# Block sums of the Winograd weights: summed on GpSimd, or added up by transfers out of HBM

## The chip, the cores and the metric

The kernel runs on one core of one Trainium2 chip. The metric is device microseconds of that core, from one launch. Three runs of the kernel before took 2677.23, 2677.38 and 2682.13 us; the median is 2677.38 us. Engines are named as in the profile: PE (TensorE), DVE (VectorE), ACT (ScalarE), POOL (GpSimd) and SP (SyncE, which here does nothing but issue transfers).

## The reference, cut to what matters

The model is one step of a two-layer trunk with 128 context and 512 latent tokens (640 columns), width 1024. Each layer is a half-step SwiGLU FFN, a token mixer, and another half-step FFN, so the FFN runs four times. Only the FFN's first two products are touched by the change:

```
def _ffn_half(x, mod, slot, w1, w3, w2, g, b):
    h = _modulate(x, mod[:, 3 * slot], mod[:, 3 * slot + 1])
    f = (jax.nn.silu(h @ w1) * (h @ w3)) @ w2
    return _residual_post_norm(x, f, mod[:, 3 * slot + 2], FFN_RES, g, b)
```

`w1` and `w3` are 1024 x 2816 in fp32, `w2` is 2816 x 1024.

## The kernel before, in words

**Precision.** Every fp32 product is made of three fp32r products: high half of the weight by high half of the activation, high by low, low by high. So each weight block first becomes two tiles: `wh` is the cast on ACT (line 299), `wl` the difference of the fp32 block and `wh` (line 306, called "low" below). Lines 299 and 306 run for each block of 128 x 512 elements, and there are six places (SLOTS) for such pairs of tiles, which go round: a block is cast when the product five places ahead of it is about to be issued, and its place is free once the product before that one has ended.

**The FFN's order.** The 22 column blocks of `w1` and `w3` are taken in chunks of 4, 3, 3, 4, 4 and 4. After each chunk comes a stage with `w2`: eight output blocks, each from as many k-blocks as the chunk has columns. The first three column blocks of an FFN are computed plainly; the other 19 as a *pair* (w1's and w3's block together) in the Strassen-Winograd form. Per FFN that is one pair in the first chunk, three in each of the next two and four in each of the last three, 76 pairs in the whole kernel.

**A pair.** The two weight blocks, each 1024 x 128, are cut into a11, a12 (w1) and a21, a22 (w3), each 512 x 128, or 128 partitions x 512 elements. The activations are cut in the same way and their sums t1 to t4 stand ready for the whole FFN. Seven products take the place of eight: p1 = a11 b11, p2 = a12 b21, p4 = a22 t4, p6 = s2 t2, p7 = s3 t3, p5 = s1 t1, p3 = s4 b22, with the block sums s1 = a21 + a22, s2 = s1 - a11, s3 = a11 - a21, s4 = a12 - s2. Each product is 12 matmuls of 128 x 320. They are issued in the order of the tuple `BLOCKS`: a11, a12, a22, s2, s3, s1, s4.

**Who makes the sums.** `Stream.load` lets SP fetch a pair as two transfers of 512 KB into two raw buffers. `Stream.combine` has POOL make the four sums out of them (line 259) just as the first of them is to be cast; they lie in four buffers `ws` (pool `pt`). The lows of s2 and s4 are made by POOL (`ON_POOL`), all others by DVE.

**What becomes of the products.** `Pair.run` issues the products, and each `prod` ends in `slot()`, which puts on the engines' queues what the products before have left to do. The order on DVE is thus written by hand: m = p1 (a copy on ACT, line 895), the upper left output is m + p2 (line 862, in `c11`), then m + p6, + p7, - p4, + p5 make the lower outputs ("the quarters", line 858 in the trace for all of them), `c12` adds p3, and then come silu, the gate products, and the cast and low of the result (lines 886 and 891), which the `w2` stage reads. Matmul results lie in four single banks of PSUM which go round (p1, p2, p6, p7, p3, and others) and two double ones (p4 with p5).

Every engine works through its queue in order. What waits at the head of a queue holds up all that stands behind it.

## Time and profile before

| | us |
|---|---|
| median of three runs | 2677.38 |
| the profiled execution | 2677.22 |
| its span, first to last instruction | 2675.0 |
| PE busy in it | 2537.6 (95%) |
| DVE busy | 2068.8 (77%) |
| POOL busy | 1243.9 (46%) |
| ACT busy | 1176.7 (44%) |

The clock that was granted to TensorE is 0.983 of full speed as a mean over the span. The profiled execution lasted 2.2 us longer than its span. An engine's idle time costs something only where PE waits for it; the waits of PE are listed by line and by what ended them.

### The profile page before, as it was taken

To read this page: it belongs to the slowest core of one execution; us is meant where nothing else is said; L and a number is where in the kernel's file an instruction comes from. 1 tells how busy PE (TensorE), PEld (TensorE's weight loads), DVE (VectorE), ACT (ScalarE), POOL (GpSimd) and SP (SyncE) were. 2 spreads that over 40 slices of the span, in tenths; PEclk is the share of its full clock that TensorE was granted. 3 is DMA by queue.
4 is the path that set the end of the run, shared out by engine and by line. 5 is a ranking of instruction groups with operands and counts; after the bars stand their busy time and mean duration, and the time that the engine had idled before them with its cause. 6 is when DMAs were issued, how large, how long until landed. Compare 5 with 4: busy or idle time off the path is not lost. (4 is left out here: it accounts for less than half of the span.)

```text
span 2675.0 us, 49819 instructions
## 1 busy us (share of the span) xinstructions
PE 2537.6 (95%) x18662; PEld 2437.0 (91%) x18662; DVE 2068.8 (77%) x3759; ACT 1176.7 (44%) x2596; POOL 1243.9 (46%) x973
## 2 busy tenths in 40 slices
PE   7999999899999999999989999998998999999997
PEld 6999999889778999999989999998996798999997
DVE  6589899856764879988987998898586558777776
ACT  5233333555574533333453333334555735334333
POOL 1345445522444555544565454454234456435554
PEclk9999999999999999999999999998999999999998
DMA  7333332355344233333223333323452331222222
GB/s 266 120 94 107 100 103 91 106 165 148 96 125 156 72 99 99 102 109 104 71 82 99 100 103 109 105 87 125 141 159 80 104 123 44 78 85 84 83 79 72
DMA packets 130544, 285.88 MB, mean 107 GB/s; under 512 B 16832, under 2 KB 34560, under 8 KB 129664
## 3 DMA queue, kind: packets, MB, share of 16 engines
q1 hardware_dynamic: 110720, 247.04, 29.3%
q10 hardware_dynamic: 19584, 35.66, 4.2%
q8 instruction: 148, 2.42, 0.4%
q14 instruction: 92, 0.75, 0.1%
HBM read 254.95 MB, written 8.81 MB: 99 GB/s over the span
## 5 line engine op out<-in xcount | busy, mean ns | idle before, releaser
L306 DVE TENSOR_TENSOR wl<-wr,wh 128x512 fp32r<-128x512 f32 (+1 forms) x524 | 510.0, 987 | 74.2 <-ACT wh L299 73.1
L299 ACT CAST wh<-wr 128x512 fp32r<-128x512 f32 (+1 forms) x570 | 332.7, 607 | 484.5 <-DMA wr<-in_w 309.2
L485 PE MATMUL o<-gh,wh 128*128 128x256 f32 (+1 forms) x1408 | 439.7, 312 | 19.7 <-ACT gh L886 12.1
L485 PE MATMUL o<-gl,wh 128*128 128x256 f32 (+1 forms) x1408 | 438.6, 312 | 1.8
L485 PE MATMUL o<-gh,wl 128*128 128x256 f32 (+1 forms) x1408 | 436.4, 310 | 0.0
L847 PE MATMUL p<-hh,wh 128*128 128x320 f32 x1216 | 377.1, 310 | 10.9 <-DVE pm L858 10.8
L847 PE MATMUL p<-hl,wh 128*128 128x320 f32 x1216 | 377.2, 310 | 6.6 <-DVE hl L1010 6.6
L847 PE MATMUL p<-hh,wl 128*128 128x320 f32 x1216 | 377.4, 310 | 0.7 <-DVE wl L306 0.7
L259 POOL TENSOR_TENSOR ws<-wr 128x512 f32<-128x512 f32 x76 | 110.4, 1453 | 544.8 <-DMA wr<-in_w 508.5
L299 ACT CAST wh<-ws 128x512 fp32r<-128x512 f32 x304 | 185.7, 621 | 355.1 <-PE p L847 128.4
L306 POOL TENSOR_TENSOR wl<-ws,wh 128x512 fp32r<-128x512 f32 x152 | 239.9, 1582 | 189.2 <-ACT wh L299 188.6
L610 DVE SCALAR_TENSOR_TENSOR x<-o,gat,x 128x128 f32<-128x128 f32 (+2 forms) x404 | 193.0, 525 | 137.1 <-PE o L485 135.5
L485 PEld LDWEIGHTS o<-gh,wh 128*128 128x128 f32 x1408 | 267.7, 190 | 23.4 <-ACT gh L886 15.0
L485 PEld LDWEIGHTS o<-gl,wh 128*128 128x128 f32 x1408 | 267.9, 190 | 6.8 <-DVE gl L891 4.8
L485 PEld LDWEIGHTS o<-gh,wl 128*128 128x128 f32 x1408 | 267.5, 190 | 0.0
L847 PEld LDWEIGHTS p<-hh,wh 128*128 128x128 f32 x1216 | 228.9, 188 | 13.2 <-issue 12.2
L847 PEld LDWEIGHTS p<-hl,wh 128*128 128x128 f32 x1216 | 229.1, 188 | 7.7 <-DVE hl L1010 7.7
L847 PEld LDWEIGHTS p<-hh,wl 128*128 128x128 f32 x1216 | 229.2, 189 | 1.8 <-DVE wl L306 1.5
L460 DVE SCALAR_TENSOR_TENSOR scr<-wv,cb 128x512 f32<-128x512 f32 x192 | 174.8, 910 | 0.0
L259 POOL TENSOR_TENSOR ws<-wr,wr 128x512 f32<-128x512 f32 x76 | 130.4, 1715 | 0.6 <-DVE wl L306 0.6
L259 POOL TENSOR_TENSOR ws<-wr,ws 128x512 f32<-128x512 f32 x76 | 130.4, 1716 | 0.0
L306 DVE TENSOR_TENSOR wl<-ws,wh 128x512 fp32r<-128x512 f32 x152 | 129.2, 863 | 0.0
(434 smaller groups left out, 6604.3 us busy)
## 6 DMA issues: line engine op xcount, KB each, us to landing
wr<-in_w SPq DMA_DIRECT2D x176, 512.0 KB, 4.2
wm<-in_wmod ACTq DMA_DIRECT2D x136, 256.0 KB, 3.1
wr<-in_w SPq DMA_DIRECT2D x128, 256.0 KB, 2.7
wv<-in_wmt SPq DMA_DIRECT2D x96, 256.0 KB, 4.1
wm<-in_wmod SPq DMA_DIRECT2D x56, 256.0 KB, 5.3
wr<-in_w SPq DMA_DIRECT2D x64, 192.0 KB, 2.4
wr<-in_wint SPq DMA_DIRECT2D x24, 512.0 KB, 4.3
wr<-in_wo SPq DMA_DIRECT2D x16, 512.0 KB, 3.8
```

The costliest lines, as they stand in the source:

```text
L259: G.tensor_tensor(out=o, in0=x0, in1=x1, op=op)
L299: S.copy(hl[0], src[:, c0:c1])
L306: eng.tensor_tensor(out=t2, in0=src, in1=t.bitcast(F32), op=ALU.subtract)
L460: V.scalar_tensor_tensor(out=scr, in0=w[2 * i + hf], scalar=1.0, in1=cb[:, 2 * st + hf, :], op0=ALU.mult, op1=ALU.mult, accum_out=a[:, 2 * ...
L485: PE.matmul(out[:, :cn], whl[a][:, k, :], b[:, c0:c0 + cn], start=k == 0 and i == 0, stop=k == n - 1 and i == 2)
L610: V.scalar_tensor_tensor(out=c, in0=src, scalar=gat[:, d, s:s + 1], in1=c, op0=ALU.mult, op1=ALU.add)
L847: PE.matmul(out[:, :HN], w[a][:, k, :], b[k][c], start=k == 0 and i == 0, stop=k == 3 and i == 2)
```

## The change

The four block sums are no longer computed by POOL. For each sum, SP copies one 256 KB quarter of the weights out of HBM straight into the sum's buffer, and then POOL issues transfers which add to that buffer: another quarter out of HBM, or the finished s1 out of its buffer. s3 takes a copy and one adding transfer, s1 a copy and one, s2 a copy and one (it adds s1), s4 a copy and two (one out of HBM, then s1). Since the transfers only add, the signs change: s2 = a11 + s1, s3 = a11 + a21, s4 = a12 + a11 + s1; `c12` and the quarters subtract m where they added it. The raw buffers hold only a11 with a12 (512 KB) and a22 (256 KB).

A sum is begun (`begin`) when the same sum of the pair before has been cast and its low made. The first pair of an FFN begins all four when its a11 is cast. All lows are made by DVE. The products follow in the order a11, a12, a22, s3, s1, s2, s4, so p7 and p5 come before p6, and the five quarter operations stand together behind p6. `run_first`, which nothing calls, is dropped.

```diff
-BLOCKS = ("a11", "a12", "a22", "s2", "s3", "s1", "s4")
+BLOCKS = ("a11", "a12", "a22", "s3", "s1", "s2", "s4")
...
             def pair(self, a, b):
                 r = len(self.src)
-                self.src += [(a, (KD, P)), (b, (KD, P))]
+                self.src += [(a, (KD, P)), (b[:, 4:8, :], (4, P))]
+                self.parts[r] = a[:, 0:4, :], a[:, 4:8, :], b[:, 0:4, :], b[:, 4:8, :]
                 return r
...
-            def combine(self, r):
-
-                self.lows()
-                self.load(r + 1)
-                a11, a12 = self.raw[r][:, :512], self.raw[r][:, 512:]
-                a21, a22 = self.raw[r + 1][:, :512], self.raw[r + 1][:, 512:]
-                s1, s2, s3, s4 = (ppt.tile([P, 512], F32, tag="pt", name=f"ws{uid()}") for _ in range(4))
-                for o, x0, x1, op in ((s1, a21, a22, ALU.add), (s2, s1, a11, ALU.subtract), (s3, a11, a21, ALU.subtract),
-                                      (s4, a12, s2, ALU.subtract)):
-                    G.tensor_tensor(out=o, in0=x0, in1=x1, op=op)
-                self.blocks = dict(s1=s1, s2=s2, s3=s3, s4=s4, pair=r)
+            def begin(self, nm, r):
+
+
+                d11, d12, d21, d22 = self.parts[r]
+                o = ppt.tile([P, 512], F32, tag="pt", name=f"ws{uid()}")
+                first = dict(s3=d21, s1=d21, s2=d11, s4=d12)[nm]
+                nc.sync.dma_start(out=o.rearrange("p (a b) -> p a b", b=P), in_=first)
+                for y in dict(s3=(d11,), s1=(d22,), s2=("s1",), s4=(d11, "s1"))[nm]:
+                    if isinstance(y, str):
+                        G.dma_start(out=o, in_=self.sums[r, y], accum_op=ALU.add)
+                    else:
+                        G.dma_start(out=o.rearrange("p (a b) -> p a b", b=P), in_=y, accum_op=ALU.add)
+                self.sums[r, nm] = o
...
-                            if r != self.blocks["pair"]:
-                                self.combine(r)
-                            src = self.blocks[shape]
+                            src = self.sums[r, shape]
+                            if r in self.after:
+                                self.done.append((shape, self.after[r], len(self.w)))
...
+                while self.done and self.done[0][2] < len(self.w):
+                    self.begin(*self.done.pop(0)[:2])
...
-        ON_POOL = ("s2", "s4")
+        ON_POOL = ()
...
+                p7 = bank("p7")
+                self.prod(p7, self.t3)
+                mods(1)
+                self.prod(p5, self.t1)
                 p6 = bank("p6")
...
+                def quarters():
+                    V.tensor_tensor(out=m[:, LO], in0=p6[:, :HN], in1=m[:, LO], op=ALU.subtract)
+                    op(m[:, HI], m[:, LO], p7, ALU.subtract)
                     self.g = u(pe_, f"gf{uid()}")
                     op(self.g[:, LO], m[:, HI], p4, ALU.subtract)
...
                     op(self.g[:, HI], m[:, HI], p5, ALU.add)
                     op(m[:, LO], m[:, LO], p5, ALU.add)
+                    return self.gate1
+                self.prod(p6, self.t2, quarters)
```

POOL, before, over one pair in the middle of the last FFN's last chunk: the sums s1, s2, s3, s4 in that order, then the lows of s2 and s4.

```order
L259 TENSOR_TENSOR ws5770_30189<-wr5744_30032 128x512 [waits DMAHW7_49,Pool_49]
L259 TENSOR_TENSOR ws5771_30190<-ws5770_30189,wr5743_30030 128x512 [waits DMAHW6_49,DVE_49,Pool_49]
L259 TENSOR_TENSOR ws5772_30191<-wr5743_30030,wr5744_30032 128x512 [waits DVE_49]
L259 TENSOR_TENSOR ws5773_30192<-wr5743_30030,ws5771_30190 128x512 [waits Pool_49]
L306 TENSOR_TENSOR wl5777_30202<-ws5771_30190,wh5776_30201 128x512 [waits PE_49,Activation_49]
L306 TENSOR_TENSOR wl5790_30263<-ws5773_30192,wh5789_30262 128x512 [waits PE_49,Activation_49]
```

POOL, now, over one pair there: the adding transfers of s3, s1, s2 and (two) of s4; DMAHW are the counters of SP's transfers, DMASW those of POOL's.

```order
L262 DMA ws5779_30587<-in_w13 128x512 [waits DMAHW2_49,DMASW5_49,DVE_49]
L262 DMA ws5788_30617<-in_w13 128x512 [waits DMASW7_49,DMAHW3_49,DMASW1_49,DVE_49]
L260 DMA ws5791_30638<-ws5788_30617 128x512 [waits DMAHW4_49,DMASW3_49,DVE_49]
L262 DMA ws5795_30660<-in_w13 128x512 [waits DMAHW5_49,DVE_49]
L260 DMA ws5795_30660<-ws5788_30617 128x512 [waits DMASW5_49]
```

Six computing instructions of a pair are gone from POOL and five transfers stand there, each behind a wait for a transfer before it.

SP, now, over two pairs of that chunk: for each pair the copies for s3, s1, s2, s4 of the next one (L257), then the raw blocks (L244). Numbers count up with the allocation, so ws_30469 and ws_30617 are s1 of two pairs that follow each other.

```order
L257 DMA ws_30430<-in_w 128x512 [waits DMASW0_49,DVE_49]
L257 DMA ws_30469<-in_w 128x512 [waits DMASW2_49,DMASW4_49,DMASW1_49,DVE_49]
L257 DMA ws_30488<-in_w 128x512 [waits DVE_49]
L257 DMA ws_30509<-in_w 128x512 [waits DMASW3_49,DVE_49]
L244 DMA wr_30566<-in_w 128x1024 [waits DMAHW2_49,DVE_49]
L244 DMA wr_30568<-in_w 128x512 [waits DMAHW3_49,DVE_49]
L257 DMA ws_30587<-in_w 128x512 [waits DMASW5_49,DVE_49]
L257 DMA ws_30617<-in_w 128x512 [waits DMASW6_49,DMASW7_49,DMASW1_49,DVE_49]
L257 DMA ws_30638<-in_w 128x512 [waits DMAHW6_49,DMAHW4_49,DVE_49]
L257 DMA ws_30660<-in_w 128x512 [waits DMAHW5_49,DMASW0_49,DVE_49]
```

The copy for an s1 waits for three adding transfers of the pair before: the one into its own buffer and the two that read it, of which the last is the second one into s4. SP had only raw blocks to fetch here.

DVE, now, over the end of one pair: the low of the next pair's s3, the five quarters, the low of s1, gate, `c12` (L881), the lows of s2 and s4, the second gate (L889), and `c11` of the next pair.

```order
L312 TENSOR_TENSOR wl5777_30571<-ws5748_30430,wh5776_30570 128x512 [waits DVE_49,DMASW5_49,PE_49,Activation_49]
L921 TENSOR_TENSOR pm5752_30463<-p65773_30564,pm5752_30463 128x320 [waits DVE_49,PE_49]
L866 TENSOR_TENSOR pm5752_30463<-pm5752_30463,p75768_30530 128x320 [waits DVE_49]
L866 TENSOR_TENSOR gf5782_30607<-pm5752_30463,p45763_30507 128x320 [waits DVE_49]
L866 TENSOR_TENSOR gf5782_30607<-pm5752_30463,p45763_30507 128x320
L866 TENSOR_TENSOR pm5752_30463<-pm5752_30463,p45763_30507 128x320
L312 TENSOR_TENSOR wl5781_30591<-ws5757_30469,wh5780_30590 128x512 [waits DMASW6_49,Activation_49]
L866 TENSOR_TENSOR gf5782_30607<-gf5782_30607,sl5767_30528 128x320 [waits DVE_49]
L881 TENSOR_TENSOR sl5767_30528<-p35778_30585,pm5752_30463 128x320 [waits DVE_49,PE_49]
L312 TENSOR_TENSOR wl5790_30621<-ws5760_30488,wh5789_30620 128x512 [waits DMAHW6_49,DMASW7_49,Activation_49]
L312 TENSOR_TENSOR wl5793_30642<-ws5764_30509,wh5792_30641 128x512 [waits DMASW0_49,DMASW1_49,PE_49,Activation_49]
```

Before, the quarters were spread over three products with lows between them, and two of these lows were not on this queue.

## Rows read from the trace of the kernel before

**Rows 1.** The page: busy us (share) and instructions of each engine.

```profile
PE 2537.6 (95%) x18662; PEld 2437.0 (91%) x18662; DVE 2068.8 (77%) x3759; ACT 1176.7 (44%) x2596; POOL 1243.9 (46%) x973
```

**Rows 2.** Whom PE waited for: us in total, times, longest.

```profile
PE o L485 <- ACT gh L886: 12.1, 14, 1.1
...
PE p L847 <- DVE pm L858: 10.8, 6, 1.9
...
PE p L847 <- DVE sl L858: 2.3, 4, 0.8
```

**Rows 3.** The chain that ended last: start us, us, what.

```profile
2544.83 28.11 PE o L485 x192
2572.93 49.27 PE p L847 x336
```

**Rows 4.** Windows (w2 stage, pairs): length; PE, PEld, DVE, ACT, POOL busy; PEclk; DMA share, GB/s.

```profile
2545.00:2573.00 28.00, 28.00 (x193) 28.00 (x192) 14.39 (x28) 6.53 (x13) 6.91 (x5) 1.00 0.32 104
2573.00:2622.00 49.00, 49.00 (x336) 49.00 (x335) 41.73 (x59) 22.36 (x42) 29.64 (x19) 1.00 0.23 70
```

**Rows 5.** Groups by line: POOL's sums and lows; busy, mean ns.

```profile
L306 POOL TENSOR_TENSOR wl<-ws,wh 128x512 fp32r<-128x512 f32 x152 | 239.9, 1582 | 189.2 <-ACT wh L299 188.6
...
L259 POOL TENSOR_TENSOR ws<-wr,ws 128x512 f32<-128x512 f32 x76 | 130.4, 1716 | 0.0
L259 POOL TENSOR_TENSOR ws<-wr,wr 128x512 f32<-128x512 f32 x76 | 130.4, 1715 | 0.6 <-DVE wl L306 0.6
...
L259 POOL TENSOR_TENSOR ws<-ws,wr 128x512 f32<-128x512 f32 x76 | 119.4, 1572 | 6.6 <-POOL ws L259 0.7
...
L259 POOL TENSOR_TENSOR ws<-wr 128x512 f32<-128x512 f32 x76 | 110.4, 1453 | 544.8 <-DMA wr<-in_w 508.5 <-DVE x L610 25.8 <-DVE scr L460 3.4
```

**Rows 6.** DVE's timeline: lows beside POOL's sums and without them.

```profile
2376.82 3.25 DVE L306 TENSOR_TENSOR wl<-wr,wh 128x512 fp32r<-128x512 f32 x2
2379.99 1.91 DVE L891 TENSOR_TENSOR gl<-gf,gh 128x640 fp32r<-128x640 f32 x1
...
2386.84 0.68 DVE L306 TENSOR_TENSOR wl<-ws,wh 128x512 fp32r<-128x512 f32 x1
```

**Rows 7.** POOL's timeline beside those lows.

```profile
2377.89 1.63 POOL L259 TENSOR_TENSOR ws<-ws,wr 128x512 f32<-128x512 f32 x1
```

**Rows 8.** DMA issues: queue, count, KB each, median us from issue to landing.

```profile
wr<-in_w SPq DMA_DIRECT2D x176, 512.0 KB, 4.2
...
wr<-in_w SPq DMA_DIRECT2D x128, 256.0 KB, 2.7
...
x<-xd SPq DMA_DIRECT2D x16, 320.0 KB, 5.9
```

**Rows 9.** SP's issue of a raw block: ns min/median/max.

```profile
L243 SPq DMA_DIRECT2D wr<-in_w x368: 327/328/1633, 3.5 to 2634.9; - x184
```

**Rows 10.** DVE's timeline where a chunk's pairs begin.

```profile
2572.97 1.01 DVE L610 SCALAR_TENSOR_TENSOR x<-o,gat,x 128x512 f32<-128x512 f32 x2 [2.50 <-PE o L485]
2573.90 1.28 DVE L306 TENSOR_TENSOR wl<-ws,wh 128x512 fp32r<-128x512 f32 x2
```

**Rows 11.** ACT's timeline: a cast, silu and the copy of p1.

```profile
2386.48 0.62 ACT L299 CAST wh<-ws 128x512 fp32r<-128x512 f32 x1 [1.13 <-PE p L847]
2387.01 0.47 ACT L877 ACTIVATE sl<-sl 128x320 f32<-128x320 f32 x1
2387.38 0.41 ACT L895 COPY pm<-p 128x320 f32<-128x320 f32 x1
```

**Rows 12.** DVE's timeline at a chunk's end: quarter operations, c12, the last low.

```profile
2396.66 0.48 DVE L858 TENSOR_TENSOR gf<-pm,p 128x320 f32<-128x320 f32 x1
2397.06 0.48 DVE L858 TENSOR_TENSOR pm<-pm,p 128x320 f32<-128x320 f32 x1
...
2397.86 0.48 DVE L858 TENSOR_TENSOR sl<-pm,p 128x320 f32<-128x320 f32 x1
...
2399.90 0.49 DVE L891 TENSOR_TENSOR gl<-gf,gh 128x320 fp32r<-128x320 f32 x1 [0.53 <-ACT gh L886]
```

More of the change, by code (lines that the diff above doesn't have):

```diff
@@ L224, in __init__ @@
                 self.src, self.raw, self.jobs, self.w, self.n, self.late = [], [], [], [], 0, []
-                self.eng, self.blocks = V, {"pair": None}
+                self.eng, self.parts, self.sums, self.after, self.done = V, {}, {}, {}, []
             def tile(self, ap, shape, place=None):
@@ L270, in convert @@
                             self.load(r + i)
-                            src = self.raw[r + i][:, :512] if shape == "a11" else self.raw[r + i][:, 512:]
-                        else:
-                            if r != self.blocks["pair"]:
-                                self.combine(r)
-                            src = self.blocks[shape]
+                            src = self.raw[r][:, 512:] if shape == "a12" else self.raw[r + i][:, :512]
+                            if (r, "s3") not in self.sums:
+                                for nm in BLOCKS[3:]:
+                                    self.begin(nm, r)
+                        else:
+                            src = self.sums[r, shape]
+                            if r in self.after:
+                                self.done.append((shape, self.after[r], len(self.w)))
                         if self.jobs[len(self.w) - 1][1] == "a22":
@@ L872, in c12 @@
             def c12(self, p3):
-                self.op(self.sl[:, HI], self.m[:, LO], p3, ALU.add)
+                V.tensor_tensor(out=self.sl[:, HI], in0=p3[:, :HN], in1=self.m[:, LO], op=ALU.subtract)
                 return self.silu2
@@ L924, in run @@
                 self.prod(p3, self.b22, lambda: self.c12(p3))
-            def run_first(self, mods, other, ts):
-                m, op = self.m, self.op
-                self.start()
-                mods(0)
-                other.start()
-                p3 = bank("p3")
-                self.prod(p3, self.b22, None, ws.get(4))
-                w22 = ws.get(0)
-                p45, p6, p7 = dbl("p4"), bank("p6"), bank("p7")
-                p4, p5 = p45[:, 0, :], p45[:, 1, :]
-                wq = [ws.get(0), ws.get(0), ws.get(2), w22]
-                for k in range(4):
-                    for o, w, b in zip((p5, p7, p6, p4), wq, (self.t1, self.t3, self.t2, self.t4)):
-                        self.mms(o, w, b, k)
-                    mods(k)
-                    next(ts, 0)
-                slot()
-                def post():
-                    self.g = u(pe_, f"gf{uid()}")
-                    op(m[:, LO], m[:, LO], p6, ALU.add)
-                    op(m[:, HI], m[:, LO], p7, ALU.add)
-                    op(self.g[:, LO], m[:, HI], p4, ALU.subtract)
-                    op(self.g[:, HI], m[:, HI], p5, ALU.add)
-                    op(m[:, LO], m[:, LO], p5, ALU.add)
-                    later.append(self.gate1)
-                    return self.c12(p3)
-                later.append(post)
         LO, HI = slice(0, HN), slice(HN, T)
@@ L2024, in trunk_kernel @@
                         r = ws.pair(*tw)
+                        if j > NC:
+                            ws.after[r0] = r
+                        r0 = r
                         for nm in BLOCKS:
```

9 lines of the change are left out of this document (removed).

## The prediction, made before the result was known

> **What bounds the kernel now.** First the busy shares: PE is busy for 95% of the span, DVE 77%, POOL 46% [rows 1]. The reader should see that there is little idle time to win on PE: 2675.0 - 2537.6 = 137 us in all. Next, whom PE waited for. Of the waits that the change can touch, three are named: 12.1 us for the cast of a chunk's last gated result (ACT gh), 10.8 us for quarter operations on DVE and 2.3 us for the sums with p2 and p3 [rows 2]; together 25.2 us, all at DVE's pace. No wait for a block sum by POOL appears there. Third, the chain that ended last: in the last FFN it is PE alone, 49.27 us for the 336 matmuls of four pairs and 28.11 us for a w2 stage [rows 3]. So a pair lasts 49.27 / 4 = 12.32 us and a product a seventh of it, 1.76 us. The windows of those two stretches show PE busy throughout at a granted clock of 1.00, that is 2.4 GHz [rows 4]. As long as every weight is cast in time, the pairs' time is set by PE, and the change doesn't take a matmul away. All depends on whether the sums are still there in time.
>
> **Part one: what goes from POOL.** Per pair four sums, 1.453 + 1.572 + 1.715 + 1.716 = 6.46 us, and two lows of 1.582 us: 9.62 us of 12.32, or 730.5 us over 76 pairs [rows 5]. PE waits for none of it, so by itself it gives nothing. What it gives is on DVE: two lows beside POOL's sums took 3.25 us and one low of a result 1.91 us, one low with POOL idle 0.68 us [rows 6, 7]. DVE gets the lows of s2 and s4, 2 x 0.68 = 1.36 us a pair, and is relieved of about 2 x (1.62 - 0.68) = 1.9 us where it met POOL. DVE comes out no fuller, with the slow operations gone. I let that take half of the 25.2 us above: 12.6 us. The ends are 0 (the waits have another cause: DVE is still full while it also makes modulation vectors) and 25.2.
>
> **Part two: what is added.** Per pair SP issues six transfers in place of two and POOL five. SP's issue takes 0.33 us [rows 9], 2 us a pair, hidden, as SP computes nothing. The trace has no adding transfer and none issued by POOL. Three durations are needed.
> - The copy of 256 KB, c: 2.7 us, the row of just that size [rows 8].
> - An adding transfer of 256 KB from issue to landing, a. It can't be less than a copy of its size, 2.7 us. The longest row near it is 5.9 us for 320 KB [rows 8]. It has to read the quarter and the buffer, 512 KB, and the row for 512 KB is 4.2 us: I take 4.2.
> - POOL's own time for an issue that stands ahead of another, i: between SP's 0.33 us [rows 9] and 1.7 us, POOL's instruction on a block of that size [rows 5]; I take the middle, 1.0.
>
> By the Trainium skill (Collectives: The Full Stack, "The bandwidth ceiling: the fold count and why AG ≠ RS ≠ AR") an add in a transfer is free as arithmetic but needs two source reads on the same ring, which halves the rate. That agrees with pricing it as 512 KB; no run here shows it yet.
>
> **The loop through s1 and s4.** The new order of SP shows what "begun one pair ahead" is bound to: the copy for s1 of the next pair waits until the second adding transfer into s4 of this pair, which reads s1, has landed. In between, POOL's queue is in order: add to s1 (a), then issue s2's add, which waits for s1 and is itself issued (i), then s4's first add (a), then s4's second, which waits for the first (a). From one s1 copy to the next, then, at least
>
> C = c + a + i + a + a = 2.7 + 4.2 + 1.0 + 4.2 + 4.2 = 16.3 us,
>
> and a pair takes 12.32. The sums fall behind by 4.0 us a pair; what covers it is the start a chunk gives them. Count from the beginning of a chunk's first product. The low of s1 of the first pair is made behind the last residual of the w2 stage: 2573.90 + 0.64 = 2574.54, that is 1.6 us after 2572.93 [rows 3, 10]; with a hand-over, s1 of the second pair starts at 1.7. So s4 of pair k has landed at 1.7 + (k - 1) C. Its product is the seventh, 6 x 1.76 = 10.56 us after the pair's beginning, and ahead of it ACT must cast s4 (0.62) and then, as they stand behind that cast, do a silu (0.47) and copy p1 (0.41), whose bank this product takes [rows 11]: s4 must have landed 9.0 us after the pair's beginning. Pair k is late by (k - 1)(C - 12.32) - 7.3: pair 2 not, pair 3 by 0.7 us, pair 4 by 4.6 us. A chunk of three pairs loses 0.7, one of four 4.6. The w2 stage of 28.1 us [rows 3] then lets the sums catch up, so each chunk begins anew. In four FFNs: 12 x 4.6 + 8 x 0.7 = 60.8 us.
>
> The FFN's first pair begins all its sums when a11 is cast, two plain column blocks ahead (each 48 matmuls at 28.11 / 192 = 0.146 us, 7.0 us): 14 + 9 = 23 us of cover against i + C = 17.3. No loss.
>
> **Part three: what is moved.** The five quarters now stand together behind p6. At a chunk's end p6 ends 1.76 us before the pairs' end at about 2396.9; quarters follow each other every 0.40 us, so five and the gate take 2.4 us and c12 could start at 2397.6 to 2397.9, against 2397.86 now, and the last low would end as now at about 2400.4 [rows 12]. I cost it at nothing; the cover is the 0.9 us that c12 waits on DVE today anyway, and with a low ahead of the quarters it would be 0.7 us for each of 20 chunks, 14 us. p7's bank is now held until the second quarter, 0.8 us after p6's end; its next user, p2 of the next pair, comes 3.5 us after it. SP's raw blocks stand behind copies that wait: the fourth pair's go out when s4 of the second is cast and its low made, at 18.0 + 1.3 = 19.3 us, and land by 24; their cast is due five places ahead, at 36.96 - 8.8 = 28.2. Hidden, with 4 us to spare; beyond it the copy waits with s4, in the same loss.
>
> **Sum.** The profiled execution took 2677.22 us, of which its span is 2675.0; that is 0.16 us under the median of the runs. 2677.22 + 60.8 - 12.6 = 2725.4: 2725 us, 1.8% slower.
>
> **Rivals.**
> - *The loop fits.* With C up to 12.32 + 7.3 / 3 = 14.75, that is a up to 3.7 us, no pair is late; only the relief of DVE is left: 2665 us, at best 2677.2 - 25.2 = 2652. For it: a is then nearer to the row for 256 KB, 2.7 us, and while POOL issues, nothing else of its own is in the way. Against: four transfers in a chain leave 0.9 us apiece above the plainest copy. The Trainium skill (DMA: Bandwidth & Descriptors, "Anatomy of one DMA — SWDGE (gpsimd) path") fits a transfer issued by POOL as about 2.0 us plus the bytes at 436 GB/s; for 262144 bytes that is an estimate of 2.6 us, which would put the case here. No row shows such a transfer.
> - *The transfers crowd each other.* A pair moves 0.79 MB raw and 1.05 MB of copies, and five adds of 0.26 MB: 3.15 MB if an add counts once, 4.46 if twice. The engines' rate at full share is 70 / 0.23 = 304 to 104 / 0.32 = 325 GB/s [rows 4], 3.7 to 4.0 MB in 12.32 us. Counted twice, the load doesn't fit, and transfers stretch to the longest row, 5.9 us [rows 8]. Then C = 2.7 + 1.0 + 17.7 = 21.4, pair 3 is late by 10.9 and pair 4 by 19.9: 12 x 19.9 + 8 x 10.9 = 326 us, 2991 us. Against: the chain by itself keeps only two or three transfers in flight.
> - *It isn't a pair ahead at all.* If the copies were held by SP behind raw blocks, s3 would be late as well; the order on SP puts the copies first, so I give it nothing beyond the case above.
>
> **Chances and range.** Forecast (a between 3.7 and 5.2): 0.44. The loop fits: 0.37. Crowding: 0.19. The measurement can tell 0.2%, 5.4 us, from no change. Of the second case 0.06 falls within 0.2%, and 0.04 of the first, where the late pairs and the relief cancel: same 0.10. Faster is the rest of the second case, 0.31 less 0.01 for the quarters' cost: 0.30. Slower 0.60. The range goes from 2652, the whole relief, to a = 5.2: C = 19.3, pair 3 late by 6.7 and pair 4 by 13.6, 217 us less the relief: about 2880. For the forecast alone, a from 3.7 to 5.2, it is 2665 to 2880.
>
> **What would show it.** Right: casts of ws on ACT that end idle time by a transfer (ws from POOL's queue), at s4 and mostly in the third and fourth pair of a chunk; PE waiting at p3 for that cast; last FFN's four-pair stretches of 53 to 55 us in place of 49.27; a landing of 4 us or so for the transfers that L260 and L262 issue; single lows on DVE near 0.68 us. Wrong: no PE wait for ws at all (then the loop fits), or waits at s3 and s1 too and transfer engines busy beyond 0.8 (crowding), or a PE wait for gh that grows by more than 0.5 us a chunk (then the quarters cost what I left out).

## The result, and the profile after

The changed kernel takes 3075.61 us (median of four runs, 3069.07 to 3079.36) against 2678.82 us: a ratio of 1.147 [1.145, 1.149]. The prediction was 2725 us with a range up to 2880, so the direction was right, and the place of most of the loss; the size was not, and the range missed too: 48 us slower were forecast, 397 came. The profiled execution has a span of 3077.6 us, 402.6 more than before.

Busy shares after, to be held against [rows 1]:

```profile
PE 2688.7 (87%) x18662; PEld 2537.5 (82%) x18662; DVE 1875.2 (61%) x3911; ACT 1164.8 (38%) x2596; POOL 835.9 (27%) x897
```

PE does the same 18662 matmuls, is idle for 389 us in place of 137, and is busy 151 us longer. DVE, with 152 more instructions, is busy 194 us less. Whom PE waited for, as in [rows 2]:

```profile
PE p L855 <- ACT pm L903: 156.4, 50, 5.6
PE p L855 <- ACT wh L305: 27.4, 26, 1.7
PE p L855 <- DVE pm L921: 25.8, 21, 2.1
PE o L493 <- DVE pm L921: 20.9, 15, 2.9
PE o L493 <- ACT gh L485: 19.9, 19, 1.8
```

The first row is the wait that the prediction described: p3 takes p1's bank, and the copy of p1 stands on ACT behind the cast of s4, which has not landed. The fourth and fifth are in the w2 stage, where I had expected next to nothing. The same windows as [rows 4], in the last FFN (two four-pair stages, each with the w2 stage behind it, and the last one; columns as there):

```profile
2759.48:2826.89 67.41, 56.83 (x338) 54.09 (x338) 31.97 (x59) 20.21 (x39) 14.43 (x17) 0.89 0.68 160
2826.89:2857.87 30.98, 29.94 (x192) 28.96 (x192) 17.59 (x35) 7.82 (x14) 2.80 (x4) 0.97 0.52 134
2857.87:2925.86 67.99, 55.12 (x338) 52.52 (x338) 31.98 (x59) 20.21 (x39) 14.58 (x17) 0.94 0.67 156
...
2956.90:3022.36 65.46, 54.09 (x338) 51.97 (x338) 31.89 (x59) 20.22 (x39) 12.90 (x15) 0.96 0.62 140
```

Four pairs take 65.5 to 68.0 us in place of 49.4, and PE is busy for only 54 to 57 of them. The w2 stage takes 31.0 us in place of 27.95, two thirds of that as longer matmuls (29.94 us busy for the same 192). The granted clock is 0.97, so part of it ran at 1.2 GHz, behind PE's wait for the last pair; 3% of 31 us is 0.9 us, half of what the matmuls are longer. Within the pairs the clock isn't what sets the length: at 0.89, 0.94 and 0.96 the three stages differ by 2.5 us, and not in the order of the clock. PE's waits in them are at p3 alone but for some 1 us a stage, none of them at s1 or s3, and the share of the transfer engines is 0.62 to 0.68: the prediction's signs of crowding are absent. What sets it is in the chain of waits, here one turn from one late s4 to the next (start us, us, what):

```profile
2974.69 3.35 DMA ws<-ws
2978.14 0.63 ACT wh L305
...
2982.52 5.97 DMA ws<-in_w
...
2989.04 0.84 POOL ws L260
2989.89 0.89 POOL ws L262
2990.77 4.00 issue
2994.79 3.32 DMA ws<-ws
2998.21 0.63 ACT wh L305
```

and SP's queue in between, the copies for the next pair:

```profile
2978.11 1.74 SPq L257 DMA_DIRECT2D ws<-in_w  x3
```

It is the loop of the prediction: s1's copy is issued when the transfer of 2974.69 has landed (2978.1) and lands at 2982.5; the add to s1 lands at 2988.5; behind it POOL issues s2's add and s4's first add, which lands at 2994.8; s4's second add lands at 2998.1. One turn is 2998.21 - 2978.14 = 20.1 us; I had worked out 16.3. Three others in the last FFN's last two chunks take 19.4 to 20.4 us from one cast of s4 to the next.

The transfers' issues (columns as in [rows 8]), and POOL's queue (q0: packets, MB, share of 16 engines):

```profile
q0 software_dynamic: 54720, 99.64, 19.4%
...
ws<-in_w SPq DMA_DIRECT2D x304, 256.0 KB, 4.2
ws<-in_w POOLq DMA_DIRECT2D x228, 256.0 KB, 5.0
...
ws<-ws POOLq DMA_DIRECT2D x152, 256.0 KB, 3.3
```

DVE's lows of the sums, the second half of the forecast (busy us, mean ns):

```profile
L312 DVE TENSOR_TENSOR wl<-ws,wh 128x512 fp32r<-128x512 f32 x304 | 206.6, 689 | 511.5 <-ACT wh L305 511.2
```

A low of a sum takes 689 ns as a mean: the 0.68 us of the quiet stretches in [rows 6].

**Where the 402.6 us are.** Adding up the 24 pair stages of each trace (from the first start to the last end of their matmuls) splits the span in two:

| kernel | pair stages | rest of the span | median us |
|---|---|---|---|
| before | 984.2 | 1690.8 | 2678.8 |
| after | 1291.1 | 1786.5 | 3075.6 |
| order alone (e1_order) | 1042.4 | 1666.0 | 2708.7 |
| order, lows on DVE (e1b) | 998.2 | 1676.1 | 2677.2 |
| lows on DVE alone (e9) | 969.8 | 1691.7 | 2666.5 |
| s4 from s2 (e2) | 1091.4 | 1794.2 | 2892.9 |
| plain copies (e3) | 1051.4 | 1796.8 | 2850.0 |
| s1 in own buffers, last FFN (e5) | 1246.4 | 1797.0 | 3043.4 |
| chunk by chunk (e8) | 1433.3 | 1738.9 | 3173.0 |
| chunk by chunk, s4 from s2 (e11) | 1136.4 | 1755.3 | 2895.9 |
| w2 in own buffers, last FFN (e12) | 1289.1 | 1763.6 | 3051.0 |
| s4's first add ahead (e18) | 1058.4 | 1849.2 | 2912.8 |
| that and w2 in own buffers (e20) | 1064.2 | 1833.6 | 2902.8 |
| s3 alone by transfer (e14) | 955.5 | 1715.8 | 2672.7 |
| the same, begun later (e21) | 963.1 | 1696.9 | 2660.6 |

The change lost 306.9 us in the pairs and 95.7 us outside them, 83 of these in the 20 stretches between two pair stages of an FFN, which are its w2 stages: 4.2 us each.

### The profile page after: what moved, and what is told of

Its sections match the earlier page's. It is cut to its first block, busy times and chain, and to the rows that moved or that the text cites. A ratio compares the mean times of both kernels' runs of the same rounds, so it can differ in the third digit from the quotient of the medians.

```text
span 3077.6 us, 50980 instructions
## 1 busy us (share of the span) xinstructions
PE 2688.7 (87%) x18662; PEld 2537.5 (82%) x18662; DVE 1875.2 (61%) x3911; ACT 1164.8 (38%) x2596; POOL 835.9 (27%) x897
## 3 DMA queue, kind: packets, MB, share of 16 engines
q0 software_dynamic: 54720, 99.64, 19.4%
## 5 line engine op out<-in xcount | busy, mean ns | idle before, releaser
L855 PE MATMUL p<-hh,wh 128*128 128x320 f32 x1216 | 411.1, 338 | 182.4 <-ACT pm L903 156.4
L312 DVE TENSOR_TENSOR wl<-ws,wh 128x512 fp32r<-128x512 f32 x304 | 206.6, 689 | 511.5 <-ACT wh L305 511.2
L312 DVE TENSOR_TENSOR wl<-wr,wh 128x512 fp32r<-128x512 f32 (+1 forms) x524 | 379.2, 740 | 157.1 <-ACT wh L305 156.6
L262 POOL DMA_DIRECT2D ws<-in_w x228 | 236.4, 1041 | 799.6 <-DVE wl L312 439.0
L855 PE MATMUL p<-hl,wh 128*128 128x320 f32 x1216 | 402.3, 331 | 1.3 <-DVE hl L987 1.3
L855 PE MATMUL p<-hh,wl 128*128 128x320 f32 x1216 | 401.7, 330 | 0.0
L260 POOL DMA_DIRECT2D ws<-ws x152 | 129.6, 853 | 753.4 <-DMA ws<-in_w 575.9
L468 DVE SCALAR_TENSOR_TENSOR scr<-wv,cb 128x512 f32<-128x512 f32 x192 | 131.2, 683 | 0.0
L855 PE MATMUL p<-tq,wh 128*128 128x320 f32 x456 | 117.5, 312 | 0.0
L855 PE MATMUL p<-tva,wh 128*128 128x320 f32 x304 | 74.1, 325 | 27.8 <-ACT wh L305 27.4
```

Source lines behind the costliest of these rows:

```text
L260: G.dma_start(out=o, in_=self.sums[r, y], accum_op=ALU.add)
L262: G.dma_start(out=o.rearrange("p (a b) -> p a b", b=P), in_=y, accum_op=ALU.add)
L312: eng.tensor_tensor(out=t2, in0=src, in1=t.bitcast(F32), op=ALU.subtract)
L468: V.scalar_tensor_tensor(out=scr, in0=w[2 * i + hf], scalar=1.0, in1=cb[:, 2 * st + hf, :], op0=ALU.mult, op1=ALU.mult, accum_out=a[:, 2 * ...
L855: PE.matmul(out[:, :HN], w[a][:, k, :], b[k][c], start=k == 0 and i == 0, stop=k == 3 and i == 2)
```

## The experiments

**1. The order alone** (sums and lows on POOL as before, products and quarters as in the changed kernel).

```diff
-BLOCKS = ("a11", "a12", "a22", "s2", "s3", "s1", "s4")
+BLOCKS = ("a11", "a12", "a22", "s3", "s1", "s2", "s4")
...
+                    V.tensor_tensor(out=m[:, LO], in0=p6[:, :HN], in1=m[:, LO], op=ALU.subtract)
...
```

> The order of the products and the quarters alone: the four sums on POOL again (as additions, in the order s3, s1, s2, s4), the lows of s2 and s4 on POOL as before. If the loss comes from the sums that are added up by transfers, this runs as the kernel before does: 2677 us, within 8 us (no PE wait for a cast of ws, four pairs in 49.4 us in the last FFN). If the quarters, standing together behind p6, are part of the loss, it is slower by up to 14 us, with more PE wait for gh than 12.1 us; if they were the main cause, it would be near 3075.

Measured: 2708.71 us, ratio 1.011 [1.009, 1.013], 29 us slower and so beyond the 8 and the 14 us expected. In the last FFN nothing is lost (every stage as before); the loss is in the three FFNs that also make modulation vectors. There PE waits for a PSUM bank until DVE gets to the quarters.

**2. The order with the lows of s2 and s4 on DVE**, as the changed kernel has them (`ON_POOL = ()` on top of experiment 1).

> The new order of products and quarters, sums on POOL as before, but with the lows of s2 and s4 on DVE, as the changed kernel has them: the order's price where POOL makes no lows. Theory order: the quarters standing together cost 30 us by themselves, through PSUM banks held until DVE gets to them; less the 13 us that the lows on DVE gave alone it is 2690 to 2700, with PE's wait 'p behind DVE pm' still 25 us or more. Rival: it was DVE, slowed beside POOL's lows, that couldn't follow; with these gone the order is free: 2662 to 2675.

Measured: 2677.16 us, ratio 1.0006 [0.9994, 1.0018]: neither 2690 to 2700 nor 2662 to 2675. PE's wait for the quarters, first with the lows on POOL, then on DVE:

```profile
PE p L846 <- DVE pm L912: 47.3, 20, 3.7
```

```profile
PE p L846 <- DVE pm L912: 25.1, 16, 2.2
```

Half of the wait came from DVE being slow beside POOL's lows; the other half stays. Against experiment 3, which differs from this one in the order alone (of products, quarters and POOL's sums), the order costs 1.0006 - 0.9944 = 0.6%, some 16 us, give or take 6 by the two intervals.

**3. The lows alone on DVE**, in the kernel before.

```diff
-        ON_POOL = ("s2", "s4")
+        ON_POOL = ()
```

> The kernel before, with the lows of s2 and s4 on DVE in place of POOL; sums, order and quarters as before. It is the part of the change that I expected to relieve DVE, alone. Theory relief: DVE meets POOL less, its lows beside POOL get shorter, PE's waits for DVE shrink: 2660 to 2675. Rival, DVE is simply given 152 lows more (152 x 0.69 = 105 us) while POOL's sums still slow it: waits for pm and gh grow, 2685 to 2710. The relief of the changed kernel would then come from the sums that left POOL, not from the lows.

Measured: 2666.46 us, ratio 0.9944 [0.9924, 0.9964]: faster than before by 15 us.

```profile
L306 DVE TENSOR_TENSOR wl<-wr,wh 128x512 fp32r<-128x512 f32 (+1 forms) x524 | 478.8, 929 | 79.6 <-ACT wh L299 78.6
...
L306 DVE TENSOR_TENSOR wl<-ws,wh 128x512 fp32r<-128x512 f32 x304 | 249.5, 836 | 1.0 <-ACT wh L299 0.5
```

152 lows more should add 152 x 0.69 = 105 us to DVE; its busy time goes from 2068.8 to 2074.8. The lows fall from 987 and 863 ns to 929 and 836, and together still grow by 89 us (639.2 to 728.3); the rest is taken back by DVE's other instructions, as by the gate product `gf<-gf,sl` of line 858 (776 to 484 ns) and the low of the gated result (1147 to 931 ns). **With the low of s2 alone moved** (`ON_POOL = ("s4",)`) it is half the step:

> The kernel before, with only the low of s2 on DVE (that of s4 stays on POOL). Half the step of the run with both lows on DVE: relief 2668 to 2677, the rival 2680 to 2695.

Measured: 2672.09 us, ratio 0.9968 [0.9951, 0.9985], within the 2668 to 2677 of the relief.

**4. One add fewer in the loop** (s4 = a12 + s2 in place of a12 + a11 + s1).

```diff
-                for y in dict(s3=(d11,), s1=(d22,), s2=("s1",), s4=(d11, "s1"))[nm]:
+                for y in dict(s3=(d11,), s1=(d22,), s2=("s1",), s4=("s2",))[nm]:
```

> The changed kernel with s4 = a12 + s2: one adding transfer in place of two, and s1 is no longer read for s4. Loop theory: the copy of the next s1 now waits only for s2's add, so the loop is copy 4.4 + add 6.0 + 0.5 + add 3.3 = 14.2 us in place of 20, and s4 lands 3.4 us after s2. s4 of pair k lands at 1.7 + 17.5 + (k - 2) 14.2 us after the chunk's first product and is due at 9.0 + 12.32 (k - 1): late by nothing, nothing, 1.6 us for pairs 2 to 4. So 20 us over the kernel less some relief of DVE: 2670 to 2710 us, and the granted clock back at 0.97 or more. Crowding theory: the bytes of a pair, adds counted twice, fall from 4.46 to 3.94 MB, by 12%; landings shorten by as much, the loop from 20 to 17.6 us, and pairs 3 and 4 are late by 3.3 and 8.6 us: 130 us and something for the clock, 2830 to 2880 us.

Measured: 2892.89 us, ratio 1.081 [1.078, 1.084]. Both ranges are missed. The pair stages give back 200 us of the 307; by its terms the loop theory expected 254 - 20 = 234, crowding 254 - 130 = 124. The last FFN's four-pair stages take 56.0, 55.6 and 52.8 us, where the loop theory gives 51 and crowding 58. So this run leans to the loop but, as it takes bytes away as well, doesn't decide. The rest of the span gives back nothing (1794 against 1786 us): both theories took the pairs for the whole loss.

**5. s1 in buffers of its own, last FFN only** (the same bytes and adds, but s1's copy needn't wait for s4).

```diff
+                if nm == "s1" and r in self.own:
+                    o = pm.tile([P, 512], F32, tag="wm", name=f"ws{uid()}")
...
```

> The changed kernel, but in the last FFN alone s1 takes its turn in four other buffers, which lie idle there: its copy no longer waits for the adds into s4 of the pair before. All transfers, bytes and their order on each queue are the same. Loop theory: the period is then set by POOL's queue in order (add to s1 6.0, issues 0.5 and 0.5, first add to s4 5.2, two issues 2.1: 14.3 us), pair 4 is late by 4 us in place of 15.8: the last FFN's four-pair stretches fall from 65.5 to 68 us to 53 to 56, three-pair ones from 45 to 47 to about 40; in all about 50 us less, 3025. Crowding theory: nothing is taken off the transfer engines, so the stretches stay at 65 us and more, and the time at 3075.

Measured: 3043.4 us, ratio 1.136 [1.133, 1.139]. The first and last of its four-pair stages in the last FFN, the last at full clock:

```profile
2746.71:2808.64 61.93, 53.92 (x338) 53.14 (x338) 31.70 (x59) 20.03 (x39) 14.96 (x18) 0.92 0.76 172
...
2932.83:2987.47 54.64, 50.39 (x339) 49.43 (x339) 30.91 (x59) 20.04 (x39) 12.60 (x15) 1.00 0.71 157
```

67.4, 68.0 and 65.5 became 61.9, 59.0 and 54.6; with the traffic even higher (DMA share 0.71 to 0.78). So the hand-over from s4 to s1 is a cause, and volume alone isn't. The first two stages stayed above the 53 to 56 us expected, and the time above the 3025: that FFN's pair stages gained 32 us, its w2 stages lost 6.

**6. The same transfers without adding** (POOL's five are plain copies; the sums are then not sums).

```diff
-                        G.dma_start(out=o, in_=self.sums[r, y], accum_op=ALU.add)
+                        G.dma_start(out=o, in_=self.sums[r, y])
```

> The changed kernel with POOL's five transfers as plain copies (nothing is added, so the sums are not sums): the same issues, waits and destinations. If an adding transfer is slow because it reads the buffer too, the landing out of HBM falls from 5.0 us to 3.5 or so and that out of s1's buffer from 3.3 to 2.5, the packet time of POOL's queue falls from 6.0 us per MB to the 3.2 of SP's queue, the loop from 20 to about 15 us, and the kernel to 2690 to 2740 us. If it is slow because POOL issues it, landings stay at 5 and 3.3 us and the time near 3075.

Measured, in a single run: 2849.95 us.

```profile
q0 software_dynamic: 30400, 99.64, 10.7%
...
ws<-in_w POOLq DMA_DIRECT2D x228, 256.0 KB, 3.9
...
ws<-ws POOLq DMA_DIRECT2D x152, 256.0 KB, 2.3
```

For the same 99.64 MB the adding transfers held the engines 0.194 x 3077.6 / (0.107 x 2848.2) = 1.96 times as long, and each landed 1.0 to 1.1 us later: it is mostly the adding that is slow, not the issue by POOL. The time is above the expected 2690 to 2740 us: the pair stages give back 240 us, the rest of the span nothing. The Trainium skill (Collectives: The Full Stack, "The bandwidth ceiling: the fold count and why AG ≠ RS ≠ AR") says of the reducing step of a collective that its add needs two source reads and so halves the rate. In engine time the traces agree with what the prediction made of it for an adding transfer. The Trainium skill's other figure that I had used as a rival, 2.6 us for 256 KB issued by POOL (DMA: Bandwidth & Descriptors, "Anatomy of one DMA — SWDGE (gpsimd) path", an estimate), isn't met here out of HBM, where even the plain copy takes 3.9 us, with other transfers in flight; a lone one was not measured.

**7. The w2 stage: SP's queue?** My first theory for the longer w2 stages was that w2's loads stand on SP behind copies of the next chunk's first sums. So these sums were begun only at their own a11.

```diff
-                        if j > NC:
+                        if j > max(NC, j0):
                             ws.after[r0] = r
```

> The changed kernel, but the sums of a chunk's first pair are begun when that pair's own a11 is cast (as an FFN's first pair already does it), not behind the last pair of the chunk before. So SP issues no sum copy that waits at a chunk's end, and the w2 blocks' loads go out at once. Theory SP queue: the 4.7 us by which each of the 20 w2 stages is longer than before come from w2 loads that stand behind a copy of s1 that waits for its buffer (then: the cast, DVE in order, the quarters, PE). Then the last FFN's w2 stages fall from 32.7 to about 28 us, PE's wait 'o behind DVE pm' goes, the pair stages stay at 65 to 68 and 45 to 47 us or 1 us longer, and the time is 3075 - 94 = 2980, up to 2995. Rival, the quarters at a chunk's end or the transfers' traffic make the w2 stages longer: they stay at 32.7 us and the time at 3060 to 3080.

Measured: 3172.97 us, ratio 1.182 [1.178, 1.186]: slower by 97 us. The expected time fell, and in the last FFN's four-pair chunks so did the theory: w2 stages there still take 30.1 and 29.8 us (31.0 in the changed kernel; the 32.7 us named in the expectation belongs to the run with s4 from s2). But the 20 w2 stages together went from 606.3 to 561.7 us, with 523.2 before: half of their loss is gone. Where it is gone entirely is the first w2 stage of each FFN (113.4 us over four, as before; 128.5 in the changed kernel). The last FFN's, first in the changed kernel, with a row of POOL's timeline there, then here:

```profile
2581.02:2614.86 33.84, 29.99 (x193) 29.49 (x192) 21.29 (x36) 7.95 (x14) 9.36 (x11) 0.95 0.45 117
...
2592.08 7.04 POOL L813 TENSOR_SCALAR x<-x,deriv 128x640 f32<-128x640 f32 x8
```

```profile
2652.15:2680.09 27.94, 27.94 (x193) 27.94 (x192) 15.18 (x32) 6.79 (x12) 3.45 (x4) 1.00 0.63 167
```

In the changed kernel the adds of the next pair stand there on POOL ahead of the scaling of x, which then runs beside a low on DVE of 4.41 us; experiment 10 meets the same again. Which part of it is SP's queue, as the theory has it, and which POOL's, this run can't tell. The four-pair stages grew to 74 to 78 us, since all sums of a chunk are begun later:

```profile
2908.52:2938.58 30.06, 29.78 (x194) 29.01 (x193) 17.65 (x35) 7.80 (x14) 2.84 (x4) 0.97 0.52 153
2938.58:3014.24 75.66, 57.85 (x338) 54.77 (x338) 31.62 (x59) 19.79 (x39) 14.40 (x17) 0.90 0.61 134
```

With s4 taken from s2 as well:

> Both edits together: s4 is a12 plus s2 (one adding transfer fewer a pair), and a chunk's first pair begins its sums at its own a11. If the loop and the SP queue are two causes of their own, the gains add: 2893 - 94 = about 2800 (2785 to 2815), with four-pair stages of 52 to 56 us and w2 stages of 28 us in the last FFN. Rival, the two are one cause (the queue waits only because the loop is late): once the loop is shorter there is less to win, 2840 to 2890.

Measured: 2895.92 us, ratio 1.079 [1.076, 1.082], no gain on experiment 4 and above both ranges: its 20 w2 stages fell by 33 us in all (the last FFN's four-pair ones by 1.3 us, 32.7 to 31.4), its pair stages grew by 45 us. Head start and w2 stage pull against each other.

**8. The w2 stage: the raw buffers.** The chain at a chunk's end in the changed kernel shows another reason:

```profile
2917.53 3.30 DMA ws<-ws
...
2920.93 0.63 ACT wh L305
...
2922.99 0.70 DVE wl L312
2923.71 3.23 DMA wr<-in_w
...
2927.03 0.63 ACT wh L305
...
2928.41 3.36 DMA wr<-in_w
...
2931.87 0.62 ACT wh L305
2932.48 0.37 ACT gh L485
```

The late s4 is cast at 2920.93. The first two w2 blocks are cast behind it, though they had been loaded long before; only with their lows do the two raw buffers come free, a load takes 3.2 us, and the next two need 3.4 us more. DVE's lows stand ahead of the chunk's last quarters, and on ACT the fifth block's cast ahead of gh, for which PE waits. In the last FFN four buffers of 256 KB are free, and w2's blocks were given these:

```diff
+                    if len(self.raw) in self.own:
+                        r = pm.tile([P, 512], F32, tag="wm", name=f"wr{uid()}")[:, :shape[0] * shape[1]]
...
-                            self.load(r + 3)
+                            self.load(r + 5 if r + 2 in self.own else r + 3)
```

> The changed kernel, but in the last FFN the w2 blocks are loaded into four buffers of their own (free in that FFN), and the first four of a stage are asked for with the last pair's a22; elsewhere they share the two raw buffers with the pairs. Theory raw buffers: a w2 stage is 4.7 us longer because its first two raw blocks are cast behind the late s4, the third and fourth can be loaded only after that (2.7 to 3.4 us of landing), and their lows stand ahead of the chunk's last quarters on DVE. Then the last FFN's five w2 stages fall from 32.7 to 28 to 29.5 us (each by 3.2 to 4.7), the four-pair stages stay at 65 to 68, other FFNs stay, and the time is 3075 minus 16 to 24: 3051 to 3059. Rival, DVE or the quarters' own order make the stage longer: 32.7 us stay, 3070 to 3080.

Measured: 3050.97 us, ratio 1.140 [1.137, 1.144], 25 us less than the changed kernel.

```profile
2806.75:2834.80 28.05, 28.05 (x194) 28.05 (x193) 16.64 (x34) 6.77 (x12) 2.67 (x4) 1.00 0.49 131
2834.80:2904.35 69.55, 56.31 (x338) 53.31 (x338) 32.09 (x60) 21.08 (x41) 13.85 (x17) 0.91 0.66 156
2904.35:2932.99 28.64, 28.64 (x192) 28.64 (x192) 17.27 (x35) 7.00 (x13) 3.45 (x4) 0.97 0.52 137
```

The stages are back at 28.05 and 28.64 us with PE busy throughout, while the pairs stay as late as they were. In the last FFN's four w2 stages with the edit, 14 of 17 us are gone, so there the two raw buffers are the cause of most of it. (The edit also asks for the third and fourth block earlier on SP's queue; the chain above, in which their load goes out as a low ends, speaks for the buffers.) The edit doesn't touch the w2 stage behind the FFN's first pair, which stays long (35.6 us, 33.8 in the changed kernel); that one is experiment 7's.

**9. The same transfers in another order.** s4's first add needs no s1, yet stands on POOL behind s2's add, which waits for it. Here POOL issues it first; bytes, copies and adds are the same.

```diff
-                for y in dict(s3=(d11,), s1=(d22,), s2=("s1",), s4=(d11, "s1"))[nm]:
+                self.sums[r, nm] = o
+                for t, y in dict(s3=(("s3", d11),), s1=(("s1", d22),), s2=(), s4=(("s4", d11), ("s2", "s1"), ("s4", "s1")))[nm]:
+                    o = self.sums[r, t]
...
```

> The changed kernel with the same copies and adding transfers, to the byte, but POOL issues s4's first add (which needs no s1) ahead of s2's add, which waits for s1; so it runs beside s1's add and not behind it. Theory loop: from one s1 copy to the next there are then c + a + i + a(s1 into s4) = 4.4 + 6.0 + 1.6 + 3.5 = 15.5 us in place of 20.0; a fourth pair is late by 3 x (15.5 - 12.3) - 7.3 = 2 us in place of 16, a third not at all in place of 8. The last FFN's four-pair stages fall from 65 to 68 to 53 to 55 us, three-pair stages from 45 to 47 to 38, and the time to 2840 to 2880. Rival, the transfers' volume sets the pace (the bytes and adds are unchanged): stages and time stay, 3060 to 3085.

Measured: 2912.80 us, ratio 1.088 [1.085, 1.091].

```profile
2615.01:2670.30 55.29, 51.70 (x339) 49.46 (x339) 31.28 (x59) 20.23 (x39) 13.72 (x16) 1.00 0.80 186
2670.30:2705.71 35.41, 31.68 (x194) 30.73 (x192) 18.28 (x36) 7.91 (x14) 3.41 (x4) 0.90 0.48 130
```

The pair stages lose 232.7 us by an order alone; the expectation's terms give 12 x 14 + 8 x 8 = 232. That shows the loop most clearly, at a DMA share of 0.80. The last FFN's four-pair stages take 55.3, 58.5 and 53.6 us, the middle one above the 53 to 55 expected. The time missed its 2840 to 2880, because 63 us are given back outside the pairs, in w2 stages of 34.5 and 35.4 us. With w2's blocks in their own buffers as well:

> POOL's order with s4's first add ahead (2912.8 us), and in the last FFN the w2 blocks in four buffers of their own. Theory raw buffers: that FFN's w2 stages were 29.7, 30.1, 35.4 and 34.5 us against 20.9, 20.9, 28.0 and 28.0 before; they fall to within 1 us of these, about 8.7 + 9.2 + 7.4 + 6.5 and some 4 in the last one, 36 us in all: 2870 to 2885. Rival, the adding transfers' traffic makes the w2 loads late: less than half of that is won, 2895 to 2915.

Measured: 2902.79 us, ratio 1.083 [1.080, 1.087], so the total missed its 2870 to 2885. In the place of the edit the theory holds in the main:

```profile
2673.51:2702.63 29.12, 28.98 (x193) 28.12 (x192) 18.08 (x36) 7.71 (x14) 3.41 (x4) 1.00 0.53 140
```

Both four-pair chunks' w2 stages take 29.1 in place of 35.4 and 34.5 us, the three-pair ones 23.2 and 23.3 in place of 29.7 and 30.1: 25 of the 32 us. The FFN's last four pair stages took back 5 of them, and stretches that the edit doesn't touch came out longer in this execution. That the raw buffers carry most of it is shown for these four stages. Why the w2 stage grows when the pairs get faster is open in part: with the shared buffers the stage of 35.4 us has a granted clock of 0.90, so 3.5 of the 7.5 us by which it is longer than before are time at 1.2 GHz, behind PE's waits; with buffers of its own it is at 1.00.

**10. s3 alone by transfer.** The kernel before, lows on DVE, and of the sums only s3 (which is in no loop) copied and added; the signs as in the change.

```diff
+            def begin(self, r):
+                o = ppt.tile([P, 512], F32, tag="pt", name=f"ws{uid()}")
+                v = o.rearrange("p (a b) -> p a b", b=P)
+                nc.sync.dma_start(out=v, in_=self.parts[r][1])
+                G.dma_start(out=v, in_=self.parts[r][0], accum_op=ALU.add)
+                self.s3[r] = o
...
```

> A version meant to beat both: the kernel before with its order, lows of s2 and s4 on DVE, and of the four sums s3 alone by transfer (one copy, one adding transfer, begun when s3 of the pair before has its low); s1, s2 and s4 on POOL. No loop binds it: s3's buffer waits for s3's low alone, 10 us ahead of its next use at the least. Theory fits: POOL does 1.6 us less a pair, DVE's lows beside it get shorter, no PE wait for ws: 2655 to 2666. Rival, POOL's queue is held by the add that waits for its copy and s1's sum comes late: 2670 to 2700. It also measures c and a where little else moves (two transfers a pair): if the other transfers stretched them in the changed kernel, c is here about 2.7 and a 3.5 to 4.2 us; if they are so long by themselves, 4.0 and 5.0.

Measured: 2672.65 us, ratio 0.9979 [0.9962, 0.9995], in the rival's range. Every four-pair stage of every FFN is now at 49.43 us, but the w2 stage behind an FFN's first pair went from 27.9 to 34.4 to 35.1 us in three FFNs. POOL's and DVE's timelines there:

```profile
2260.85 0.86 POOL L244 DMA_DIRECT2D ws<-in_w  x1 [10.87 <-DVE wl L317]
2261.49 7.01 POOL L818 TENSOR_SCALAR x<-x,deriv 128x640 f32<-128x640 f32 x8
```

```profile
2263.52 5.53 DVE L317 TENSOR_TENSOR wl<-wr,wh 128x512 fp32r<-128x512 f32 x1 [2.36 <-ACT wh L310]
```

The add waits at the head of POOL's queue, 10.87 us for the low that frees its buffer and for its copy; the scaling of x stands behind it and then runs beside a low, which takes 5.53 us in place of 0.69 and ends at 2269.05, just after the scaling (2268.50). So POOL's queue is held as the rival had it, but what comes late is not s1's sum. The transfers' rows, where little else moves:

```profile
wr<-in_w SPq DMA_DIRECT2D x128, 256.0 KB, 2.7
...
ws<-in_w SPq DMA_DIRECT2D x76, 256.0 KB, 3.9
ws<-in_w POOLq DMA_DIRECT2D x76, 256.0 KB, 4.1
```

**With the second chunk's first s3 begun at its own a11**, so that no add stands ahead of the scaling:

```diff
-                        if j > NC:
+                        if j > CHUNKS[0][1]:
```

> The version with s3 alone by transfer (2672.65 us), but the second chunk's first pair begins its s3 at its own a11, so no add stands in POOL's queue ahead of the scaling of x at an FFN's first pair. Theory POOL queue: there a w2 stage of 28 us took 34.4 to 35.1 in three FFNs, with a low on DVE of 5.53 us beside POOL's scaling; these 7 us each go, less the 3 to 4 us that the one pair ahead of it gained: 2652 to 2666. Rival: the stage stays at 35 us and the time at 2668 to 2677.

Measured: 2660.57 us, ratio 0.9926 [0.9906, 0.9947], and those stages are back at 27.94 us. It beats both kernels: by 0.7% the one before, by 13% the changed one. But most of the 0.7% is already in experiment 3, which moves only the lows (0.9944 [0.9924, 0.9964]); the intervals overlap, so it isn't shown that the transfer of s3 adds anything to that.

## Why the prediction was wrong, step by step

Two steps of the sum failed most: the sizes in the loop, a C of 16.3 us where 20.0 were measured, and the w2 stages, for which it had no term and which cost 83 us.

- **What bounds the kernel** (PE, as long as every sum is cast in time): right. With the sums in time, as in the last experiment, four pairs take 49.44 us again.
- **The loop through s1 and s4:** right as a mechanism, down to the place of the wait, p3 behind the copy of p1 behind the cast of s4. It failed in the sizes. In C = c + a + i + a + a, at the turn shown above, the copy was 4.4 us in place of 2.7, the add into s1 6.0 in place of 4.2, the issue 1.1 in place of 1.0, s4's first add 5.2, its second 3.3: 20.0 in place of 16.3. Each late pair pays the difference again: 3.7 us of C turned the 60.8 us into 12 x 15.8 + 8 x 8.1 = 254 us by the same formula. It also gives 49.3 + 15.8 = 65.1 us for a four-pair stage, and 65.5 to 68.0 were measured in the last FFN.
- **Why c was too small:** I took the row for 256 KB of w2. With almost no other transfers a sum's copy takes 3.9 us beside that same 2.7 (experiment 10); it is issued 1.6 to 3.5 us behind two raw blocks there, which may be why (not tried by itself). **Why a was too small:** 4.1 us is right where little else moves, 4.2 had been taken; among the other transfers it became 5.0, and 6.0 for the one in the loop.
- **The rival "the transfers crowd each other"** was right that a would stretch: its C of 21.4 is nearer to the measured 20.1 than the forecast's, though its 2991 us are still too low. But the volume doesn't set the pace, as experiments 5 and 9 show.
- **SP's raw blocks, "hidden with 4 us to spare":** for the pairs' blocks this held, since the casts became late with the loop as well: in none of the 20 stages of three or four pairs does a cast of a raw block wait for its transfer (an instance stands below this list). What failed is that the step looked at the pairs' blocks alone: w2's blocks share the two raw buffers and are cast behind the late s4. The 20 w2 stages grew by 83 us, of which the sum held nothing. The raw buffers are shown for the last FFN's four w2 stages behind three and four pairs (14 of 17 us, and 4 more behind the last pair stage); that it is the same in the other three FFNs is inferred. The w2 stages behind the FFNs' first pairs (15 of the 83 us) have another cause: their loss goes when the next chunk's sums are begun later (experiment 7).
- **The quarters, costed at nothing (up to 14 us):** they cost 16 us by the difference between experiments 2 and 3, in PSUM banks held in the three FFNs that also make vectors, not in gh at a chunk's end, where I had looked.
- **DVE's relief, 12.6 us:** experiment 3 gives 15 us, but for another edit: there only the lows left POOL, and all four sums stayed. What the relief is worth in the changed kernel no run separates, so the agreement is luck as far as the runs show; half of 25.2 was a choice.
- **Clock:** no term for it in the sum. Stretches at 1.2 GHz stand behind PE's waits. By the granted clock of each, the 20 w2 stages lose about 37 us to them, 1.9 us each (0.9 in the one shown above), and none before: a part of the 83 us. In the pairs, where more is lost (98 us, 10 before), I take it that the loop hides them. The clock wasn't tried by itself.
- **The FFN's first pair, "no loss":** it takes 20.7 to 21.8 us in place of 18.2 to 19.1, 11 us in four; why wasn't looked into.

In the pairs 254 of the loop, 14 of the order with the lows on DVE (998.2 - 984.2) and 11 in the FFNs' first pairs leave some 28 of the 306.9 us unexplained, 21 of them in the FFNs that also make vectors.

The instance of raw blocks in time: in the last FFN's last chunk but one the fourth pair's are asked for at 2884.46, and two of them are cast right behind the late s4 of the third pair, with no wait of their own:

```profile
2901.52 0.62 ACT L305 CAST wh<-ws 128x512 fp32r<-128x512 f32 x1 [5.13 <-DMA ws<-ws]
...
2902.72 1.14 ACT L305 CAST wh<-wr 128x512 fp32r<-128x512 f32 x2
```

## What to carry to other kernels

Where work begun ahead hands a buffer round, write the cycle down and compare its length with the period: an excess of 4 us is paid again with every turn, and an error in one term of it is multiplied likewise. Take a term's duration from a row with the same neighbours, not only the same size, and look at which waits at the head of an in-order queue could be issued later: an order that put the one independent add first gave back 233 us in the pairs, though 63 of them were lost again in the stages behind, 163 us in all being left. When a late item is the last of a stage, follow the shared buffers into the next stage too.

## What the runs showed of the hardware

- An adding transfer out of HBM holds the engines about twice as long as a plain one (1.96 times over all of POOL's), but with little else moving it takes only 0.2 us more to land than a copy issued by SP (4.1 against 3.9 us, experiment 10); among the changed kernel's transfers the difference is 1.1 us (5.0 against 3.9 for POOL's plain ones, experiment 6).
- POOL is busy for the issue of an adding transfer 0.85 us (out of SBUF) to 1.04 us (out of HBM) as a mean, and 0.54 us for a plain one.
- A low on DVE took 5.53 us beside POOL's scaling of x, and 0.69 us as a mean in the changed kernel, where POOL computes no sums: the same instruction, eight times as long. It ended 0.55 us after the last of eight scalings in a row, and so did the one of 4.41 us in the changed kernel (2599.67 after 2599.12), as if it had waited for all of them. 152 lows that went from POOL to DVE made DVE 6 us busier.
